# A two-layer FoX and RetNet trunk on one core: accumulator banks and small tiles handed over at other blocks, and a few vector operations fewer

## The chip, the core and the metric

The kernel runs on one core of one Trainium2 chip. The metric is the device time in microseconds (us). An engine is named by its short form: PE is the matrix engine, DVE the vector engine, ACT the scalar engine, POOL GpSimd, SP the engine that issues most DMAs.

## The reference, cut

One sequence of 512 tokens, width 2048, passes two layers; all is fp32.

```python
def fox_branch(x, w_in, b_f, q_gain, k_gain, w_out):
    q, k, v, gate, f_logit = split(x @ w_in)             # 16 heads of 128
    q = rms_norm(heads(q), q_gain); k = rms_norm(heads(k), k_gain)
    c = cumsum(log_sigmoid(f_logit + b_f))               # "forget", per head
    s = q @ k.T * 128 ** -0.5 + c[:, None] - c[None, :]  # causal mask
    return (softmax(s) @ v * silu(gate)) @ w_out

def retention_branch(x, w_in, w_out):
    q, k, v, gate = split(x @ w_in)                      # 8 heads, qk 256, v 512
    q, k = rotary(q), rotary(k) * 256 ** -0.5
    o = retention(q, k, v)                               # decayed chunks of 128 tokens
    return (group_norm_heads(o) * silu(gate)) @ w_out

for i in range(2):
    y = fox_branch(h, ...) if i == 0 else retention_branch(h, ...)
    h = layer_norm(ALPHA * h + y, ln_gain[i], ln_bias[i])
```

## The kernel before

**Products.** An fp32 product is three matmuls (`mm3`, L307 to L309): each operand is split into a high and a low part, the weights by ACT (`w_h`, L302) and DVE (`w_l`, L303). Almost all of the time goes into products of a 512 x 2048 operand with a piece of weights 1024 columns wide ("wide") or 512 ("narrow"). A `Unit` does such a product in Strassen's manner with seven products p1 to p7; a `Plain` unit does it without, in quarters (m, n) (m is the token half, n the column half). Each product is a few blocks: a wide block is 12 matmuls of 128 x 512, a narrow one 24 of 128 x 256. There are 750 blocks; below they are counted from 0 in the order in which PE runs them.

**Accumulators.** PSUM is dealt out by hand: three accumulators of two banks each (`b0` to `b2`, which a unit calls x, y, z) and two small one-bank tiles, `mmp`, for everything else (transposes, scores, a tanh). In a `Unit`, p6, p7 and p4 share x: L457 reads x after p7's last block, and p4 goes on in x after that. p3 has z, read by L452. A tile's next user waits for its last reader.

**Order.** All engines run their instructions in program order, and a planner (`Order`) writes that order. It walks along the list of blocks. Behind each block's matmuls it emits the small steps (generators that `yield need(...)`) that are due: a step is due a given number of blocks after the one before it (`wait`, else 1), when its rings are free (`mmp`, `tmp`, `st` and others are counted with `take` and `give`; `give(ring, 1)` frees it a block later), and while the work booked for DVE and ACT (`debt`) stays under `LIMIT` = 4.4 and 3.8. Weights are loaded up to 9 blocks ahead by SP; the split of a block is emitted three blocks ahead of it, in three buffers.

**What runs where.** Blocks 0 to 15 are a plain narrow unit (q and k of heads 0 and 1), 16 to 43 the first wide unit (`vg[0]`), 44 to 211 nine more such units, narrow (q and k of two heads) and wide (values and gates), with the attention of twelve heads behind them; 212 to 227 a plain narrow unit, 228 to 291 the plain units of FoX's output projection, whose sums are added to the residual by `add_z` (L1373); from 292 on retention, and its output projection to the end. The last unit runs `EARLY`: p4 is cut in two token halves of four blocks each, the "last tokens" second.

Steps that the change touches: `Pair.take` copies a finished narrow quarter (ACT, L956) and takes sums of squares in place (L961); `forget` makes the gates c with 96 matmuls of 16 columns on an `mmp` tile; `silu_twice` (L853, L855) computes a tanh in an `mmp` tile; `head` does a head of attention, transposes of the weights L1035, product L1180, copy by ACT L1186, gate transposes L1190, gating L1193; `rsqrt_steps` is three Newton steps of tiny DVE operations; `first_stores` and `last_stores` normalise and write the output.

## Time and profile before

| what | value |
| --- | --- |
| time, median of 3 runs | 2407.43 us (2407.38 to 2410.28) |
| the profiled execution | 2409.79 us, its span 2408.0 us |
| busy share of the span | PE 97%, DVE 79%, ACT 51%, POOL 6% |
| mean granted clock of PE | 0.992 |
| chain that ended last | PE 71%, DVE 14%, ACT 5%, issue 5%, DMA 4% |

The profiled execution is 1.8 us longer than its span. Views give for each engine when an instruction started, how long it took, how long the engine was idle before it and which instruction ended that idle time. The granted clock is the share of full speed that the throttle gave PE in a stretch; its two levels are 1.2 and 2.4 GHz. Line numbers are those of the kernel before.

### The profile page before, as it was taken

Reading aid. Unit: us, or ns where it says so; the run is one execution under the profiler, and the core shown is the slowest. Engines: PE = TensorE matmul, PEld = TensorE weight load, DVE = VectorE, ACT = ScalarE, POOL = GpSimd, SP = SyncE. Lnnn points to the kernel's source line nnn. Section 1 sums busy time; section 2 is a strip of 40 time slices with the busy share of each in tenths; the row PEclk is TensorE's granted clock in tenths of the full one; section 3 lists DMA queues with packets and bytes.
Section 4 is the critical chain, followed back from the end, with each engine's and each line's share of the span. In section 5 each row is a group of like instructions: output and inputs, shape, how many; then the busy total and the mean of one; then the engine's idle time right before and its main releaser. Section 6 shows DMA issues by size and latency. Waiting matters only on the chain.

```text
span 2408.0 us, 34403 instructions
## 1 busy us (share of the span) xinstructions
PE 2334.7 (97%) x13144; PEld 2023.4 (84%) x13144; DVE 1896.8 (79%) x2506; ACT 1221.5 (51%) x1777; POOL 150.5 (6%) x237
## 2 busy tenths in 40 slices
PE   9999999999999999999999999999999999999995
PEld 9788898789789778878989898888889898777784
DVE  4878778768765556677888888898888889987977
ACT  4546556556555534565453545454544446554543
POOL 0000000000000000000010101010101001011002
PEclk9999999999999999999999999999999999999998
DMA  5445554544544457656585857665665659689777
GB/s 212 140 159 171 179 171 153 185 157 154 177 161 144 141 180 233 220 167 206 197 241 188 243 191 220 204 197 184 209 198 191 211 169 274 208 266 299 240 247 176
DMA packets 185142, 473.27 MB, mean 197 GB/s; under 512 B 18033, under 2 KB 63233, under 8 KB 184465
## 3 DMA queue, kind: packets, MB, share of 16 engines
q1 hardware_dynamic: 161296, 403.42, 50.9%
q0 software_dynamic: 23680, 67.66, 10.6%
q8 instruction: 103, 1.69, 0.3%
q14 instruction: 63, 0.51, 0.1%
HBM read 413.30 MB, written 61.91 MB: 197 GB/s over the span
## 4 chain that ended last, share of the span: by engine, by line
PE 71%; DVE 14%; ACT 5%; issue 5%; DMA 4%; POOL 0%; ACTq 0%; DVEq 0%; SPq 0%; POOLq 0%
PE acc L308 21%; PE acc L307 21%; PE acc L309 21%; DVE w_l L303 5%; DMA w_raw<-in_wide 3%; ACT w_h L302 3%; DVE w_q L551 3%; PE mmp L307 2%; PE mmp L308 2%; PE mmp L309 2%; PE mmp L1180 1%; PE mmp L1035 1%; DVE qk_l L987 0%; DVE w_raw L547 0%; DMA y_s<-ny 0%
## 5 line engine op out<-in xcount | busy, mean ns | idle before, releaser
L307 PE MATMUL acc<-w_h,a 128*128 128x512 f32 (+1 forms) x1616 | 584.5, 362 | 19.8 <-DVE p L457 8.2
L303 DVE TENSOR_TENSOR w_l<-w_raw,w_h 128x1024 fp32r<-128x1024 f32 x337 | 411.7, 1222 | 219.5 <-ACT w_h L302 218.0
L308 PE MATMUL acc<-w_l,a 128*128 128x512 f32 (+1 forms) x1616 | 579.2, 358 | 4.5 <-DVE w_l L303 4.4
L309 PE MATMUL acc<-w_h,a 128*128 128x512 f32 (+1 forms) x1616 | 578.5, 358 | 0.0
L302 ACT ACTIVATE w_h<-w_q 128x1024 fp32r<-128x1024 f32 x344 | 363.4, 1058 | 405.4 <-DVE w_q L551 241.5
L302 ACT ACTIVATE w_h<-w_raw 128x1024 fp32r<-128x1024 f32 x337 | 356.0, 1058 | 376.5 <-PE acc L309 197.8
L303 DVE TENSOR_TENSOR w_l<-w_q,w_h 128x1024 fp32r<-128x1024 f32 x344 | 420.1, 1222 | 95.8 <-ACT w_h L302 90.1
L307 PE MATMUL acc<-w_h,s 128*128 128x512 f32 (+1 forms) x1344 | 490.8, 365 | 1.9 <-ACT w_h L302 1.9
L308 PE MATMUL acc<-w_l,s 128*128 128x512 f32 (+1 forms) x1344 | 486.4, 362 | 6.0 <-DVE w_l L303 5.8
L309 PE MATMUL acc<-w_h,s 128*128 128x512 f32 (+1 forms) x1344 | 485.1, 361 | 0.0
L307 PEld LDWEIGHTS acc<-w_h,a 128*128 128x128 f32 x1616 | 307.7, 190 | 65.5 <-issue 13.4
L308 PEld LDWEIGHTS acc<-w_l,a 128*128 128x128 f32 x1616 | 307.9, 191 | 50.5 <-DVE w_l L303 8.7
L309 PEld LDWEIGHTS acc<-w_h,a 128*128 128x128 f32 x1616 | 307.4, 190 | 44.3
L308 PEld LDWEIGHTS acc<-w_l,s 128*128 128x128 f32 x1344 | 254.4, 189 | 48.3 <-DVE w_l L303 12.6
L309 PEld LDWEIGHTS acc<-w_h,s 128*128 128x128 f32 x1344 | 254.0, 189 | 39.3
L307 PEld LDWEIGHTS acc<-w_h,s 128*128 128x128 f32 x1344 | 254.3, 189 | 38.7 <-ACT w_h L302 2.3
L551 DVE TENSOR_TENSOR w_q<-w_q,w_raw 128x1024 f32<-128x1024 f32 x218 | 265.2, 1220 | 9.7 <-DMA w_raw<-in_wide 7.3
L307 PE MATMUL acc<-a,w_h 128*128 128x256 f32 x464 | 132.2, 285 | 1.2 <-ACT w_h L302 1.2
L309 PE MATMUL acc<-a,w_l 128*128 128x256 f32 x464 | 132.1, 285 | 0.8 <-DVE w_l L303 0.8
L308 PE MATMUL acc<-a,w_h 128*128 128x256 f32 x464 | 131.8, 284 | 0.0
L309 PE MATMUL acc<-s,w_l 128*128 128x256 f32 x448 | 126.7, 283 | 0.0
L308 PE MATMUL acc<-s,w_h 128*128 128x256 f32 x448 | 126.7, 283 | 0.0
(245 smaller groups left out, 2946.1 us busy)
## 6 DMA issues: line engine op xcount, KB each, us to landing
w_raw<-in_wide SPq DMA_DIRECT2D x343, 512.0 KB, 3.7
w_raw<-in_narrow SPq DMA_DIRECT2D x146, 512.0 KB, 3.7
w_q<-in_wide SPq DMA_DIRECT2D x60, 512.0 KB, 4.4
room<-in_wide SPq DMA_DIRECT2D x45, 512.0 KB, 4.3
w_q<-in_narrow SPq DMA_DIRECT2D x26, 512.0 KB, 4.6
y_s<-ny POOLq DMA_DIRECT2D x48, 256.0 KB, 7.3
y_s<-y POOLq DMA_DIRECT2D x40, 256.0 KB, 6.1
room<-in_narrow SPq DMA_DIRECT2D x16, 512.0 KB, 4.8
```

Of the source, the lines that this page charges most:

```text
L302: nc.scalar.activation(h, src, AF.Copy)
L303: nc.vector.tensor_sub(l, src, f32(h))
L307: nc.tensor.matmul(ps, a[0], b[0], start=start, stop=False, skip_group_check=True)
L308: nc.tensor.matmul(ps, a[0], b[1], start=False, stop=False, skip_group_check=True)
L309: nc.tensor.matmul(ps, a[1], b[0], start=False, stop=stop, skip_group_check=True)
L551: nc.vector.tensor_add(u.chain[c], u.chain[c], t)
L1035: nc.tensor.transpose(tp[g][:, at], p[q][0][:, k * P:(k + 1) * P], ident)
L1180: nc.tensor.matmul(ps[:, k * P:], vh[:, k], pT[:, k, k * P:], start=k == 0, stop=k == ST - 1)
```

## The change

- `Plain`, narrow: both column quarters of a token half are handed to their reader when both are done, no longer one by one (`PlainBlock.finish`).
- `vg[0]` alone has the ending p3, p7, p4: its last p7 block goes ahead of its last p3 block ("turned"). The piece of weights that p3 lent to p7 is then loaded at p7 and kept for p3; after a turned block DVE's limit is 2.9.
- Last unit: the last tokens' p4 accumulates in z, no longer in y after the first half's.
- `head`: the gate transposes are a step of their own, a block after ACT's copy (in the same block for the last two pairs of heads).
- `silu_twice` gives its `mmp` tile back a block later; `add_z` adds both token blocks of a quarter behind one block.
- Small operations: two multiplies of a Newton step become one where only one value per partition is treated (two uses, in `last_stores`); the copies of variances ahead of rsqrt are dropped (L1398, L1707); one more of the last stores (s = 3, c = 1) adds its bias on DVE and goes out by SP, no longer by POOL with an accumulating DMA.

```diff
@@ slot
-        self.most = (LIMIT[0], 2.4) if b.p == "p6" and b.last else LIMIT
+        self.most = (LIMIT[0], 2.4) if b.p == "p6" and b.last else (2.9, LIMIT[1]) if getattr(b, "turned", False) else LIMIT
@@ rsqrt_steps
-            nc.vector.tensor_mul(t, dst, dst)
-            nc.vector.tensor_mul(t, t, h)
+            if n == 1:
+                nc.vector.scalar_tensor_tensor(t, dst, h, dst, op0=ALU.mult, op1=ALU.mult)
+            else:
+                nc.vector.tensor_mul(t, dst, dst)
+                nc.vector.tensor_mul(t, t, h)
@@ Unit.run
+            i = order.index(("p3", self.blocks - 1))
+            if order[i + 1:i + 3] == [("p7", self.blocks - 1), ("p4", 0)]:
+                order[i:i + 2] = order[i + 1], order[i]
...
+                turned = p == "p7" and order[i + 1] == ("p3", c) or p == "p3" and order[i - 1] == ("p7", c)
@@ Block.load
+            if self.turned and self.p == "p7":
+                u.lent["p3", self.c] = t = new_raw(u.shape)
+                nc.sync.dma_start(t.rearrange("p a b -> p (a b)"), u.source("22", self.c))
@@ Block.multiply, finish
-            b = "y" if u.early and p == "p4" else BANK[p]
+            b = ("z" if self.again else "y") if u.early and p == "p4" else BANK[p]
...
-                self.u.sink(1, 0, self.u.bank["y"], lambda: self.u.leave("y") if e else None, part=1, es=(e,))
+                self.u.sink(1, 0, self.u.bank["yz"[e]], lambda: self.u.leave("yz"[e]), part=1, es=(e,))
@@ PlainBlock.finish
-            at = self.m, self.n
-            if self.u.left[at] == 0 and at in self.u.bank:
-                self.u.sink(*at, self.u.bank.pop(at), lambda after=0: self.u.leave(*at))
+            u, m = self.u, self.m
+            if u.wide or all(u.left[m, n] == 0 for n in range(2)):
+                for at in ((m, self.n),) if u.wide else ((m, 0), (m, 1)):
+                    if u.left[at] == 0 and at in u.bank:
+                        u.sink(*at, u.bank.pop(at), partial(u.leave_after, at))
@@ silu_twice
-            give("mmp")
+            give("mmp", 1)
@@ head
-            yield need(act=0.5, pe=0.45, tmp=1)
+            yield need(act=0.5, tmp=1)
             y = tmp("o")
             nc.scalar.activation(y, ps, AF.Copy, scale=0.5)
             give("mmp")
+            yield need(pe=0.45, mmp=1, wait=0 if self.quick else 1)
             g = mmp()
@@ add_z
-                        yield need(dve=1.2, until=lambda: (m, n, e) in got and o.now - got[m, n, e][1] >= 2)
+                        yield need(dve=1.2, wait=1 - e, until=lambda: (m, n, e) in got and o.now - got[m, n, e][1] >= 2)
@@ ln_factors (and the same in retain, L1707)
-        var = pool.tile([P, 2], F32, name="ln_var", tag="ln_var", bufs=2)[:, :k]
-        nc.vector.tensor_copy(var, mv[:, :, 1])
-        rsqrt(r, var, k, 1.0, LN_EPS)
+        rsqrt(r, mv[:, :, 1], k, 1.0, LN_EPS)
@@ last_stores
-            if s == 3 and c > 1:
+            if s == 3 and c > 0:
```

The planner turns these few lines into another order of small steps behind blocks 13 to 150, 178 to 205 and 210 to 325. Three places follow; line numbers in rows of the changed kernel are higher by 3 to 23.

ACT behind blocks 13 to 17, the end of the first plain unit, before:

```order
L956 ACTIVATE qk_raw<-acc 128x2x256
L302 ACTIVATE w_h<-w_raw 128x1024
L961 ACTIVATE acc,rms_ss<-acc 128x128 x4
L956 ACTIVATE qk_raw<-acc 128x2x256
L302 ACTIVATE s_624<-raw 128x1024
L302 ACTIVATE w_h<-w_raw 128x1024
L961 ACTIVATE acc,rms_ss<-acc 128x128 x4
L956 ACTIVATE qk_raw<-acc 128x2x256
```

The same place now:

```order
L305 ACTIVATE w_h<-w_raw 128x1024
L305 ACTIVATE s_620<-raw 128x1024
L305 ACTIVATE w_h<-w_raw 128x1024
L978 ACTIVATE qk_raw<-acc 128x2x256 x2
L305 ACTIVATE w_h<-w_raw 128x1024
L983 ACTIVATE acc,rms_ss<-acc 128x128 x8
L305 ACTIVATE w_h<-w_raw 128x1024
L978 ACTIVATE qk_raw<-acc 128x2x256 x2
```

The first quarter's copy no longer stands between the blocks that fill the other half of the same accumulator; both copies come after the last of them.

DVE behind the last blocks of `vg[0]` (38 to 41), before; `u` is the sum that p3's L452 makes, `p` the one that p7's L457 makes:

```order
L925 COPY fg<-fg 16x1
L926 TENSOR_TENSOR fg<-fg 16x511
L452 TENSOR_TENSOR u_1116<-acc,u_1116 128x1024
L551 TENSOR_TENSOR w_q<-w_q,w_raw 128x1024
L303 TENSOR_TENSOR w_l<-w_q,w_h 128x1024
L457 TENSOR_TENSOR p_969<-p_969,acc 128x1024
```

The same place now:

```order
L460 TENSOR_TENSOR p_1067<-p_1067,acc 128x1024
L565 TENSOR_TENSOR w_q<-w_q,w_raw 128x1024
L306 TENSOR_TENSOR w_l<-w_q,w_h 128x1024
L455 TENSOR_TENSOR u_1162<-acc,u_1162 128x1024
L565 TENSOR_TENSOR w_q<-w_q,w_raw 128x1024
```

The read of p7's accumulator stands three operations ahead of that of p3's, behind block 38, and the scan of the forget gates (`fg`) has gone to later blocks.

PE behind the first block of a narrow unit (block 142), at the gate transposes of head 6, before; under it the same transposes now (block 140):

```order
L309 MATMUL acc<-w_h,a_192 128x256
L1035 MATMUL mmp<-ident,p 128x128 x4
L1190 MATMUL mmp<-ident,by_head 128x128 x4
L307 MATMUL acc<-w_h,s_446 128x256
```

```order
L312 MATMUL acc<-w_h,a_385 128x512
L1213 MATMUL mmp<-ident,by_head 128x128 x4
L1057 MATMUL mmp<-ident,p 128x128 x3
L310 MATMUL acc<-w_h,a_418 128x512
```

The gate transposes now stand first behind their block, ahead of the other head's transposes, and the product they belong to was copied a block earlier.

## Rows read from the trace of the kernel before

**Rows 1.** The page: busy time of an engine; chain that ended last.

```profile
PE 2334.7 (97%) x13144; PEld 2023.4 (84%) x13144; DVE 1896.8 (79%) x2506; ACT 1221.5 (51%) x1777; POOL 150.5 (6%) x237
```

**Rows 2.** Waits of PE, 50 to 95 us: line, released by: total us, times, longest.

```profile
PE acc L307 <- ACT qk_raw L956: 2.2, 1, 2.2
PE acc L308 <- DVE w_l L303: 2.0, 3, 1.0
```

**Rows 3.** Timeline of DVE, the end of the first wide unit, and of PE.

```profile
141.58 1.21 DVE L452 TENSOR_TENSOR u<-acc,u 128x1024 f32<-128x1024 f32 x1
...
144.98 1.20 DVE L457 TENSOR_TENSOR p<-p,acc 128x1024 f32<-128x1024 f32 x1
146.33 0.76 PE L307 MATMUL acc<-w_h,a 128*128 128x512 f32 x1 [4.78 <-DVE p L457]
```

**Rows 4.** Stretches: us, busy PE, PEld, DVE, ACT, POOL, granted clock, DMA share, GB/s.

```profile
55.20:60.00 4.80, 4.75 (x26) 4.66 (x27) 3.50 (x3) 2.18 (x4) 0.00 (x0) 0.65 0.70 265
146.30:151.50 5.20, 5.17 (x12) 4.12 (x13) 2.15 (x2) 0.00 (x0) 0.53 (x1) 0.50 0.75 223
301.00:312.00 11.00, 8.52 (x67) 7.83 (x66) 7.72 (x11) 6.07 (x12) 0.00 (x0) 1.00 0.24 70
876.40:880.50 4.10, 4.07 (x12) 3.32 (x13) 2.00 (x3) 0.00 (x0) 0.00 (x0) 0.65 0.62 201
```

**Rows 5.** Instructions on the forget tile: min, median, max ns, first and last start.

```profile
L307 PE MATMUL mmp<-a,wf_parts x24: 276/276/283, 107.0 to 120.6; 128*16 128x256 f32 x24
```

**Rows 6.** Waits of PE, 210 to 320 us, the first two units with heads.

```profile
PE mmp L1035 <- DVE p L855: 1.5, 1, 1.5
PE mmp L1190 <- ACT o L1186: 1.5, 2, 0.7
PE mmp L307 <- ACT pT L1058: 0.9, 1, 0.9
PE mmp L1004 <- DVE o L1193: 0.4, 1, 0.4
```

**Rows 7.** Waits of PE, 400 to 510 us, the next two units with heads.

```profile
PE mmp L307 <- ACT pT L1058: 1.7, 2, 1.5
```

**Rows 8.** Waits of PE, 778 to 790 us (second plain narrow unit) and 868 to 885 us.

```profile
PE acc L307 <- ACT qk_raw L956: 1.6, 1, 1.6
PE acc L307 <- DVE z L1373: 3.1, 1, 3.1
```

**Rows 9.** Timeline of DVE at the first sums of the output projection.

```profile
872.89 0.68 DVE L1373 SCALAR_TENSOR_TENSOR z<-z_in,acc 128x512 f32<-128x512 f32 x1
...
875.61 0.68 DVE L1373 SCALAR_TENSOR_TENSOR z<-z_in,acc 128x512 f32<-128x512 f32 x1
```

**Rows 10.** Groups of DVE by line: count, busy us, mean ns, idle before.

```profile
L1707 DVE COPY gn_var<-gn_mv 128x2 f32<-128x2 f32 x16 | 2.6, 163 | 0.0
```

**Rows 11.** Timeline of PE and DVE at the end: start us, us, instruction.

```profile
2383.43 0.50 PE L307 MATMUL acc<-w_h,a 128*128 128x512 f32 x1 [3.61 <-DVE z L1378]
2383.76 0.39 PE L308 MATMUL acc<-w_l,a 128*128 128x512 f32 x1
2383.99 0.39 PE L309 MATMUL acc<-w_h,a 128*128 128x512 f32 x1
...
2386.57 0.15 DVE L1398 COPY ln_var<-ln_mv 128x1 f32<-128x1 f32 x1
2386.76 0.15 DVE L289 TENSOR_SCALAR rsq_h<-ln_var 128x1 f32<-128x1 f32 x1
...
2390.72 0.68 DVE L1378 TENSOR_TENSOR z<-z,acc 128x512 f32<-128x512 f32 x1
...
2400.64 0.69 DVE L1847 TENSOR_TENSOR z<-z,ln_last 128x512 f32<-128x512 f32 x1
```

**Rows 12.** DMA issues, 2390 to 2410 us: count, KB each, us to landing.

```profile
out<-z POOLq DMA_DIRECT2D x6, 256.0 KB, 5.2
out<-z SPq DMA_DIRECT2D x2, 256.0 KB, 5.1
```

More of the change, by code (lines that the diff above doesn't have):

```diff
@@ L512, in __init__ @@
             self.quarter = None
-            if not self.sums and not shared and p != "p1":
+            self.turned = turned
+            if not self.sums and not shared and p != "p1" and not (turned and p == "p3"):
                 self.quarter = {"p2": "21", "p3": "22", "p4": "21", "p5": "12", "p6": "22", "p7": "12"}[p]
@@ L526, in rings @@
         def rings(self):
-            return dict(q=int(self.chain), st=int(self.quarter is not None))
+            return dict(q=int(self.chain), st=int(self.quarter is not None) + int(self.turned and self.p == "p7"))
         def load(self):
@@ L545, in add @@
             if p == "p7" and not self.sums:
-                other = u.lent.pop(("p3", c))
+                other = u.lent["p3", c]
                 nc.vector.tensor_add(self.t, self.t, other)
-                end_raw(other)
+                if not self.turned:
+                    end_raw(u.lent.pop(("p3", c)))
             elif p in ("p5", "p6", "p4") and not self.sums:
@@ L566, in split @@
             else:
+                if self.turned and p == "p3":
+                    self.t = u.lent.pop((p, c))
                 raw = self.t
@@ L591, in multiply @@
             a = forms[FORM[p]]
-            b = "y" if u.early and p == "p4" else BANK[p]
-            new = u.left[p] == u.blocks and (p in ("p1", "p2", "p5") or b == "y")
-            if new and not self.again:
+            b = ("z" if self.again else "y") if u.early and p == "p4" else BANK[p]
+            new = u.left[p] == u.blocks and (p in ("p1", "p2", "p5", "p4") and b in "yz" or b == "x" and p == "p1")
+            if new:
                 u.bank[b] = u.accumulator(b)
@@ L660, in accumulator, with leave_after @@
             return t if self.wide else t[:, n].rearrange("p (e n) -> p e n", e=2)
+        def leave_after(self, at, after=0):
+            self.leave(*at)
         def leave(self, m, n):
```

10 lines of the change are left out of this document (4 added, 6 removed).

## Prediction

> **What bounds the kernel now.** I read the granted clock and the busy time of the engines first, then the chain that ended last, then PE's waits by what released them, and for each such wait the stretch behind it. PE is busy for 2334.7 of 2408.0 us [rows 1] and carries 71% of the chain. So the end can only come earlier where PE stands still, or runs slowly, for a reason that the change removes, and in the last microseconds, when PE has no work left. PE's pace is the distance of two starts, 0.23 us for 128 x 512 [rows 11], 12 of which make a wide block of 2.72 us; the 0.39 us beside it is a modelled end. A wait as the rows give it is therefore about 0.15 us shorter than what PE loses.
>
> The waits that the change can reach are few and have places. In the first 160 us: 2.2 us for ACT's copy of a quarter and three for late `w_l`, 2.0 us together [rows 2], and one of 4.78 us for L457 [rows 3]. Behind the first and the last PE ran at a granted clock of 0.65 and 0.50, its lower level of 1.2 GHz for part or all of about 5 us [rows 4]. Then the units with heads, each with several waits of 0.4 to 1.7 us [rows 6, 7], with the clock at 1.00 all the same from 301 to 312 [rows 4]. Then two single waits, 1.6 us for the same copy as at the start, 3.1 us for L1373 [rows 8], with a clock of 0.65 behind the second [rows 4]. At the end, 3.6 us for L1378 [rows 11].
>
> **First unit and vg[0], part by part.** *Quarters.* The copy of the first quarter stood between blocks that write the other half of the same accumulator. Now both copies come after the second. The 2.2 us go, and the slow stretch behind them, 4.8 x (1 - 0.65) = 1.7: **3.9**. What is late next: the accumulator is free only when two copies and eight squares are through, but its next user is block 20, four wide blocks or 10.9 us later, so nothing.
>
> *Forget's matmuls.* Because the heads' first copies come later, the planner puts the 96 small matmuls of `forget` behind blocks 21 and 22 instead of 31 and 32. They cost PE the same wherever they stand, about 11 us: from 107.0 to the last start at 120.6 [rows 5] lie all of them and one block of 2.72. But at 21 to 26 PE waited for DVE, and now DVE has those 11 us to catch up: **2.0**. The bounds are 0 and 2.0; I take all, since the catching up is five times the wait.
>
> *p7 ahead of p3.* PE waited for L457 because L452, a load sum and a split stood ahead of it on DVE, three operations, 141.58 to 144.98 [rows 3]. In the new order p7's read stands where L452 stood, ahead of them, and without the two scan operations before it. It is emitted a block earlier, and one more block (p3's last) lies between p7 and p4 on PE. If DVE is as late as it was, p7's read starts where L452 did and ends at 141.58 + 1.2 = 142.8, against p4's turn at 146.33 - 4.78 = 141.55. So between nothing and 1.2 of the 4.8 may stay; I take 0.9, since two scan operations ahead of it are gone, and the slow stretch goes, 5.2 x 0.5 = 2.6: **6.5**. p3's own read is now the late one, but z's next user is a unit away. The move issues two loads of 512 KB at one block, on SP, and every load behind them passes later through three buffers. Blocks are loaded up to nine ahead, which is the cover; without it the cost is between nothing and a block, 2.72. I take nothing. 0.3 go back for DVE's moved norms behind blocks 29 to 37. Sum of the first 160 us: 3.9 + 2.0 + 6.5 - 0.3 = **12.1**, with 8 and 14 as bounds.
>
> **Heads.** In the first two units with heads the rows sum to 4.3 us [rows 6]. Two waits are of the kind that the change is about: L1035's transposes want an `mmp` tile that `silu_twice` still reads (1.5), and the gate transposes L1190 want the copy issued just ahead of them (twice 0.75). The first goes, as the tile is given back a block later and so PE is not sent there early; the second goes, as a block of 2.7 lies between. L1004's 0.4 hangs on the same tile. The heads also move: the first gate transposes from behind block 66 to 75, so the 0.9 of L307 meets other work. I leave 1.3 of small new waits, bounds 0 and 4.3: gain **3.0**. In the two later pairs of units the same three lines recur in the same size, with L307 at 1.7 [rows 7], 5.1 each. There the order up to block 121 is unchanged, so L307's 1.7 stays; one 0.75 stays, since now other transposes (L1004) ask for the copied tile at once; and the gate transposes come behind block 123 on a tile that ACT and DVE must first empty of the next heads' q and k. Nothing in the trace shows that wait. Its nearest rows are 0.4 and 1.5 [rows 6]; I take 1.1, nearer the upper one, since two engines must finish. Left 1.7 + 0.75 + 1.1 = 3.6, gain 1.5 each: **3.1**, bounds -4 and 8. A gate step of its own also holds an `mmp` tile longer, and everything else that PE does outside accumulators is queued behind these two tiles; that is the slower rival below.
>
> **Second plain unit and output projection.** The 1.6 us [rows 8] go as in the first unit, but here block 229 takes the accumulator right behind eight squares; I leave 0.2: **1.4**, bounds 0 and 1.6. `add_z` did the second token block's sum a block later, at 875.61 against 872.89 [rows 9], and PE's next unit waited for it. Behind the first sum of 0.68 and its statistics of about the same, it starts 1.3 earlier, so 3.1 becomes 1.8. Waits of 1.5 left the clock at 1.00 [rows 4, 6], so I let the slow stretch go too, 4.1 x 0.35 = 1.4: **2.7**, bounds 1.3 and 4.5.
>
> **Small operations.** The 16 copies in retention, 2.6 us of DVE [rows 10], cost nothing and bring nothing: PE has no wait there that they end. Without that cover they would be worth 2.6.
>
> **The end.** Here DVE is the path. Its chains of tiny operations and the sums between them follow one another to 2401.3, with pauses only for ACT [rows 11], so PE's 3.6 us wait is for DVE, and taking it away by a bank that has been free since p3 brings PE's end forward, from about 2390.6 (24 matmuls from 2383.43, some slow) to 2385.1, but not DVE's. Its gain alone would be the 0.1 by which the last L1378 stood behind PE [rows 11]. The Newton chains stand on that path: one operation is 0.19 from the next [rows 11], four fewer in each of two chains are 1.5, and the copy in `first_stores` 0.2. Against it, s = 3, c = 1 adds 0.7 on DVE. Net 1.0. Both halves need each other: with the old bank, the first chain's 0.77 would end in a wait for PE. The last stores land 5.1 to 5.2 after their issue [rows 12] by either queue, and one accumulating transfer less leaves the DMA engines 0.2: **1.2**, bounds 0 and 2.5.
> The Trainium skill, "DMA: Bandwidth & Descriptors" (section "Latency and other measured facts"), gives the first byte of a transfer after some 0.6 us by the sequencers' queues and 1 us by GpSimd's; by it the end would gain 0.4 more. The trace shows 0.1 between the two [rows 12], so it is left out of the sum.
>
> **The sum.** 12.1 + 3.0 + 3.1 + 1.4 + 2.7 + 1.2 = 23.5. Some 15 waits disappear, each worth 0.15 more than its row: 2.2. Together 25.7. From the profiled execution, 2409.79, that gives 2384.1; it lies 2.4 above the median of the runs, so against the median of 2407.43 I expect **2381.7**.
>
> **Rivals.** *Heads give nothing back.* The gate transposes only change what they wait for, and the hand-over a block later meets the next user. For it: only two tiles, and all waits of the heads are for them. Against: a block of 2.7 is longer than any of these waits. Then 6.1 is missing: 2388.
> *p7's read is late all the same.* DVE was behind by more than the three operations, as its busy row shows no pause there; then the 6.5 go back: 2388. Against: fewer operations stand ahead of it now.
> *Short waits pull the clock down.* If a row of short waits is enough to bring PE to its lower level, the new order of waits behind blocks 122 to 125 could do it in four units, at 2.6 each (the price at 146 to 151): 10.4, 2392. Against: the waits before were as many, with the clock at 1.00 [rows 4].
> The Trainium skill, "TensorE: Matmul & The Clock Gate" (section "A second HAM failure mode: psum-queue depth-cycling"), describes this: cycling through PSUM banks leaves PE idle so briefly and often that its clock swings between the levels. By that rule the time would be this rival's; the row of 301 to 312 speaks against it.
> *Slower: the two small tiles jam.* The gate step keeps a tile until the block after the copy, in twelve heads. If PE then stands a whole block for a tile (2.72) and the clock falls behind it (2.6), that is 5.3 a head, 64 in all: 2446. It decides from (25.7 + 4.8) / 12 = 2.5 us a head on, more than any wait of the heads in the rows. Against: other steps can go ahead of it in the planner.
>
> **Chances.** Forecast 0.62, heads 0.16, late read 0.08, clock 0.06, several of these together so that it comes within 0.2% (4.8 us, about what a measurement of this kernel can tell from no change) 0.04, jam 0.04. The forecast's own bounds, with heads from -4 and the rest at half, are 2372 to 2391. The range for 8 in 10 is 2371 to 2395, which takes in the first three rivals. Faster by over 0.2%: 0.92; within: 0.04; slower: 0.04.
>
> **What would show it.** Right: no wait of PE for L956's successor, for p7's read at most 1 us, granted clock at 1.00 from 50 to 160 us; forget's matmuls at about 73 to 90; L1190's successor without a wait for ACT's copy in the first units; at the output projection's first sums a wait of about 1.8 with a full clock; at the end PE done 5 us before DVE's last L1378, and DVE's last operation some 15 us behind PE's last matmul. Wrong: a wait of 2 us or more for a new releaser at blocks 20 to 43 or 122 to 125, or a clock under 1.00 in a stretch where it was full.

## The result, and the profile after the change

The changed kernel took **2391.41 us** (median of 6 runs, 2388.19 to 2394.39), the kernel before, run beside it, 2408.86 us (2407.38 to 2415.09). The ratio is 0.9924, interval 0.9911 to 0.9937, so the change saved 15 to 21 us. Forecast were 2381.7 us and a saving of 25.7. The time lies in the range, the direction is right, and about a third of the expected gain is missing. The profiled execution of the changed kernel took 2388.19 us with a span of 2386.4. It is the fastest of the six, 3.2 below the median, so its stages add up to 21.6 us of gain, where the medians differ by 17.5.

The page's first part, busy time of each engine, answers [rows 1]: PE is busy 13.8 us less, with the same number of matmuls.

```profile
PE 2320.9 (97%) x13144; PEld 2016.2 (84%) x13144; DVE 1892.1 (79%) x2480; ACT 1223.0 (51%) x1777; POOL 150.4 (6%) x236
```

To see where the time went I timed each stretch of blocks on PE's timeline, from the start of the first accumulating matmul of one block to that of another. These are distances of two starts, so the modelled ends don't enter. The last column is what the prediction's sum has there. (The first 0.1 of the 21.6 is an earlier start of block 0.)

```
blocks       before    after   change   predicted
  0 to  44   152.13   141.14   -11.0      -12.1
 44 to 104   200.05   202.35    +2.3       -3.0
104 to 212   370.48   367.17    -3.3       -3.1
212 to 250   136.62   136.41    -0.2       -1.4
250 to 262    37.35    34.60    -2.8       -2.7
262 to 330   206.15   206.73    +0.6        0
330 to 726  1211.10  1206.84    -4.3        0
726 to 742    49.91    48.62    -1.3        0
742 to end    35.77    34.26    -1.5       -1.2
(modelled ends of the waits)                -2.2
```

Three places were hit (104 to 212, 250 to 262, the end), two missed by 4 us and more.

**The first 160 us.** Waits of PE in the changed kernel from 100 to 175 us (line, releaser, total, times, longest). The 2.2 us and the 4.78 us of [rows 2, 3] are gone, and from 50 to 95 us only 0.3 is left, but one wait is new:

```profile
PE acc L311 <- DVE w_l L306: 3.6, 2, 2.7
```

DVE's timeline ahead of it, and PE's first matmul behind it (start, length, instruction, idle time before and what ended it), show where it comes from:

```profile
120.88 1.22 DVE L306 TENSOR_TENSOR w_l<-w_raw,w_h 128x1024 fp32r<-128x1024 f32 x1
125.50 1.23 DVE L560 TENSOR_TENSOR w_raw<-w_raw 128x1024 f32<-128x1024 f32 x1 [3.40 <-DMA w_raw<-in_wide]
126.65 1.22 DVE L306 TENSOR_TENSOR w_l<-w_raw,w_h 128x1024 fp32r<-128x1024 f32 x1
...
127.92 0.50 PE L311 MATMUL acc<-w_l,s 128*128 128x512 f32 x1 [2.75 <-DVE w_l L306]
```

L560 at 125.50 is the load sum of the turned p7 (block 38), which needs two loads at once. SP's timeline gives their issues: the line of p3's load first, and four microseconds later the other one, when the split at 120.88 had freed a buffer.

```profile
117.87 0.33 SPq L548 DMA_DIRECT2D w_raw<-in_wide  x1
122.13 0.33 SPq L551 DMA_DIRECT2D w_raw<-in_wide  x1
```

DVE stands still for 3.40 us on the second load, the split of block 37 stands behind the sum in DVE's order, and PE waits for that split.

**The clock.** The stretches that answer [rows 4] (length, busy PE, PEld, DVE, ACT, POOL, granted clock, DMA share, GB/s): behind the first quarter, block 37, the units with heads, and the first sums of the output projection.

```profile
52.80:57.60 4.80, 4.80 (x34) 4.46 (x34) 1.40 (x2) 2.78 (x7) 0.00 (x0) 1.00 0.80 315
124.80:136.00 11.20, 8.45 (x30) 6.53 (x29) 9.94 (x11) 5.82 (x6) 0.00 (x0) 0.85 0.47 154
390.00:500.00 110.00, 105.92 (x542) 86.75 (x541) 83.21 (x140) 62.84 (x114) 5.40 (x10) 1.00 0.49 162
859.00:866.00 7.00, 5.30 (x24) 4.11 (x23) 4.92 (x6) 1.72 (x3) 0.00 (x0) 1.00 0.40 133
```

The clock is full where the quarters were and at the output projection, and under 1.00 behind the new wait of 2.75 us. That last value is one execution's: four of the kernels below have the same wait of 2.7 us at block 37, and over the 6 us behind it the clock is 0.72 in one of them (as here), 0.50 in one and 1.00 in two.

**The units with heads.** PE's waits in the first two of them, which answer [rows 6], 210 to 330 us:

```profile
PE mmp L310 <- ACT pT L1080: 1.6, 1, 1.6
PE mmp L1026 <- DVE sm L1106: 1.3, 1, 1.3
PE mmp L310 <- DVE sm L1106: 0.6, 1, 0.6
PE mmp L1057 <- ACT pT L1080: 0.6, 2, 0.3
```

L1035's wait and the gate transposes' (L1190) have gone as foreseen, but others have come, 5.0 us with the three small ones not shown, against 4.3 and a 0.2 that [rows 6] leave out. In the next two units the lines answer [rows 7]:

```profile
PE mmp L310 <- ACT pT L1080: 1.7, 2, 1.5
PE mmp L1213 <- PE acc L312: 0.9, 1, 0.9
PE mmp L1057 <- ACT pT L1080: 0.8, 3, 0.3
PE mmp L1026 <- ACT o L1208: 0.7, 1, 0.7
```

The gate transposes (L1213) wait 0.9, where the prediction had 1.1. The row names PE's own matmul, but that one had ended at 421.15. What ended the wait stands in DVE's timeline, its second read of a small tile with the next heads' q and k, which is done at 421.94; so it is the wait that the prediction meant, for a tile that ACT and DVE must first empty:

```profile
421.46 0.48 DVE L1009 SCALAR_TENSOR_TENSOR qk_l<-mmp,cols,qk_h 128x256 fp32r<-128x256 f32 x1 [0.54 <-ACT qk_h L1008]
...
422.04 0.63 PE L1213 MATMUL mmp<-ident,by_head 128*128 128x128 f32 x4 [0.89 <-PE acc L312]
```

**Second plain unit and output projection.** Waits of PE from 760 to 870 us, against [rows 8]:

```profile
PE mmp L1017 <- DVE qk_l L1009: 1.7, 1, 1.7
PE acc L310 <- DVE z L1396: 1.7, 1, 1.7
```

The 1.6 us for ACT's copy are gone. The first line is new (block 235): a split of the next activations, 1.23 us on DVE at 801.33, now stands between the q and k tiles that the transposes wait for. The second line is the 3.1 us of before, shortened by 1.4; [rows 9] had 2.72 between the two sums, now it is 1.33:

```profile
860.52 0.68 DVE L1396 SCALAR_TENSOR_TENSOR z<-z_in,acc 128x512 f32<-128x512 f32 x1
861.85 0.67 DVE L1396 SCALAR_TENSOR_TENSOR z<-z_in,acc 128x512 f32<-128x512 f32 x1
```

**The end.** PE's last matmul, DVE's last sum of an accumulator (L1401, which was L1378), two steps of a Newton chain, the first of them fused, and DVE's last operation answer [rows 11]:

```profile
2363.40 0.39 PE L312 MATMUL acc<-w_h,a 128*128 128x512 f32 x1
...
2370.10 0.68 DVE L1401 TENSOR_TENSOR z<-z,acc 128x512 f32<-128x512 f32 x1
...
2372.87 0.22 DVE L297 SCALAR_TENSOR_TENSOR rsq_t<-ln_r,rsq_h 128x1 f32<-128x1 f32 x1
2373.12 0.16 DVE L301 SCALAR_TENSOR_TENSOR ln_r<-rsq_t,ln_r 128x1 f32<-128x1 f32 x1
...
2380.05 0.69 DVE L1866 TENSOR_TENSOR z<-z,ln_last 128x512 f32<-128x512 f32 x1
```

PE is done 6.3 us before L1401 and 17 before DVE; it has no wait for the old bank any more. What the accumulating queue still does behind DVE's last operation (packets, MB, share of the 16 DMA engines), before and after, and then the stores of the last 22 us (count, KB, us to landing), against [rows 12]:

```profile
q0 software_dynamic: 322, 0.57, 49.3%
```

```profile
q0 software_dynamic: 151, 0.27, 31.5%
...
out<-z POOLq DMA_DIRECT2D x5, 256.0 KB, 5.3
out<-z SPq DMA_DIRECT2D x3, 256.0 KB, 4.7
```

### The profile page after: what moved, and what is told of

The parts are those of the page before. It is cut to its first block, busy times and chain, and to the rows that moved or that the text cites. A ratio compares the mean times of both kernels' runs of the same rounds, so it can differ in the third digit from the quotient of the medians.

```text
span 2386.4 us, 34361 instructions
## 1 busy us (share of the span) xinstructions
PE 2320.9 (97%) x13144; PEld 2016.2 (84%) x13144; DVE 1892.1 (79%) x2480; ACT 1223.0 (51%) x1777; POOL 150.4 (6%) x236
## 4 chain that ended last, share of the span: by engine, by line
PE 57%; DVE 8%; issue 3%; DMA 3%; ACT 3%; POOL 0%; ACTq 0%; SPq 0%; DVEq 0%; POOLq 0%
PE acc L311 17%; PE acc L312 17%; PE acc L310 17%; DVE w_l L306 3%; ACT w_h L305 2%; PE mmp L310 1%; DMA w_raw<-in_wide 1%; PE mmp L311 1%; PE mmp L312 1%; DVE w_q L565 1%; DMA v_sum<-in_wide 1%; PE mmp L1202 1%; PE mmp L1736 0%; DMA y_s<-ny 0%; DVE z L1835 0%
```

## The experiments

Twelve kernels were run, nine of them the changed kernel with one step (or three or four) altered, three the kernel before with one step or two added. Ratios are to the kernel before, whose median was 2407.85, 2409.13 and 2408.16 us in the three sets. A profile is one execution, and what the change doesn't touch differs between them by a microsecond or two; so the verdicts rest on stretches and waits first, and on medians where these are far enough apart. The stretches of FoX's units repeat much better: in the seven kernels that have both steps in the heads, blocks 104 to 212 took 366.99 to 367.17 us.

### p7's load sum a block later

```
-        while self.added <= min(i + 3, n - 1):
+        while self.added <= min(i + 3, n - 1) and not (getattr(b := self.line[self.added], "turned", False)
+                                                       and b.p == "p7" and self.added > i + 2):
```

> The changed kernel, but the sum of the turned p7 block on DVE is emitted one block later, behind the weight split of block 37 and no longer ahead of it. All other engines have the same order. Theory A (the new wait of 2.9 us at block 37, with 1.7 of half clock behind it, comes from this sum, which waits for the second of the turned block's two loads while the split that PE needs stands behind it on DVE): the wait at block 37 goes to under 0.5 us, the clock stays full from 120 to 136 us, the span is 3.5 to 4.6 us shorter, and the median 2387. Theory B (the three load buffers are too few once the forget matmuls stand elsewhere, so that some load is late whatever the order): the wait moves to block 38 and stays at 2 us or more, time 2391.

2388.15 us (2387.07 to 2391.59), ratio 0.9920 (0.9905 to 0.9935). The one wait of 2.7 us is gone; from 45 to 175 us PE waits in smaller pieces:

```profile
PE acc L311 <- DVE w_l L306: 2.7, 3, 1.1
PE acc L310 <- DVE p L460: 0.7, 1, 0.7
```

So the place of the sum in DVE's order was the cause of block 37's wait. Blocks 29 to 44 take 45.85 us against 46.85, however: most of the wait came back one and two blocks later, since DVE has a split and a sum for each of these blocks and is late with both. Of some 4.6 us that PE lost at block 37, about 1.0 could be had by the order; the four other kernels that keep the wait have 46.4 to 47.9 us in these blocks, the most where the clock was lowest.

### The old order of p3 and p7

```
-            i = order.index(("p3", self.blocks - 1))
-            if order[i + 1:i + 3] == [("p7", self.blocks - 1), ("p4", 0)]:
-                order[i:i + 2] = order[i + 1], order[i]
```

> The changed kernel with vg[0]'s last blocks in the old order (p3 ahead of p7), everything else as changed. Theory A (the two loads of the turned block made the wait at block 37): no wait at 36 to 38, but p4 waits for p7's read at block 40, between 1 us (DVE is less late than before) and 4.8 us with half a clock of 2.6 behind it; the time then within 3 us of the changed kernel's 2391. Theory B (buffers): the wait of 2.9 us near block 37 stays and the one at block 40 is added, time 2394 to 2398.

2390.91 us (2388.49 to 2394.66), ratio 0.9931 (0.9915 to 0.9948). No wait at block 37, but PE's wait for p7's read is back, from 45 to 175 us:

```profile
PE acc L310 <- DVE p L460: 4.2, 1, 4.2
```

Blocks 29 to 44 take 48.99 us, 2.1 more than in the changed kernel. That is what the turn is worth beside the other steps.

### The quarters handed over one by one

```
-            if u.wide or all(u.left[m, n] == 0 for n in range(2)):
-                for at in ((m, self.n),) if u.wide else ((m, 0), (m, 1)):
-                    if u.left[at] == 0 and at in u.bank:
-                        u.sink(*at, u.bank.pop(at), partial(u.leave_after, at))
+            at = m, self.n
+            if u.left[at] == 0 and at in u.bank:
+                u.sink(*at, u.bank.pop(at), partial(u.leave_after, at))
```

> The changed kernel, but a plain narrow quarter is handed over as soon as it is done, as before. Forget's matmuls go back behind blocks 31 and 32 and the heads to their old blocks. Theory A (the quarters are what moved everything in the first 320 us): the waits of 2.2 us at block 14 with 1.7 of slow clock, of 2.0 us at 21 to 26, and of 1.6 us at 226 come back, the new one of 1.7 us at 235 goes, the one at block 37 goes; and the first two units with heads, which lose 6.9 us in the changed kernel, fall to 3 us or less, as predicted for heads at their old place. Time 2390 to 2394. Rival B (the gate step brings nothing to these units wherever they stand): they stay at 6 us or more, time 2394 to 2398.

2392.63 us (2391.84 to 2394.43), ratio 0.9937 (0.9923 to 0.9952). Waits from 45 to 175 us:

```profile
PE acc L311 <- DVE w_l L306: 2.6, 5, 1.0
PE acc L310 <- ACT qk_raw L977: 2.2, 1, 2.2
PE acc L310 <- DVE p L460: 1.8, 1, 1.8
```

This is the turn without the merging. Blocks 29 to 44 take 56.30 us against 61.90 before: 5.6 for the turn in its own place, where the prediction had 6.5. The wait for p7's read is 1.8 (predicted 0.9). At block 37 there is no wait, and the turned sum's line has no idle time before it:

```profile
129.64 1.22 DVE L560 TENSOR_TENSOR w_raw<-w_raw 128x1024 f32<-128x1024 f32 x1
```

The second load is late only in company with the merged quarters. They bring forget's small matmuls forward, from [rows 5] to 72.0 to 86.1, and then these blocks follow one another every 2.7 us, where before two of them had such matmuls behind them (104 to 121 us). Blocks 44 to 104 took 198.70 us, 3.7 less than in the changed kernel. The merging, in the unit ahead, costs the units with heads their gain.

### The quarters alone

The kernel before with the merging and nothing else.

```
-            at = self.m, self.n
-            if self.u.left[at] == 0 and at in self.u.bank:
-                self.u.sink(*at, self.u.bank.pop(at), lambda after=0: self.u.leave(*at))
+            u, m = self.u, self.m
...
+            if u.wide or all(u.left[m, n] == 0 for n in range(2)):
+                for at in ((m, self.n),) if u.wide else ((m, 0), (m, 1)):
+                    if u.left[at] == 0 and at in u.bank:
+                        u.sink(*at, u.bank.pop(at), partial(u.leave_after, at))
```

> The kernel before with the merged quarters alone (both halves of a narrow accumulator are handed over together, after the second). Theory A: the merging is what cost the units with heads: it gives back the waits of blocks 14 and 21 to 26 (4.0 us in blocks 13 to 20, and 3 to 4 us net in 20 to 44 with the 11 us of small matmuls that move there), but moves the heads, so that blocks 44 to 104 become 3 us longer than in a kernel with single quarters, and block 235's new wait of 1.9 eats block 226's 1.8. Total 3 to 5 us under the kernel before. Theory B: the heads' waits are of the other steps; then blocks 44 to 104 stay within 1 us of the kernel before's 200.1 and the total is 7 us or more under it.

2400.22 us (2399.0 to 2402.64), ratio 0.9969 (0.9957 to 0.9981): 7.9 us. PE's waits from 45 to 175 us:

```profile
PE acc L307 <- DVE p L457: 4.2, 1, 4.2
```

Blocks 13 to 20 take 4.0 us less and blocks 20 to 44 5.0 less, 9.0 together where the prediction had 3.9 + 2.0. Blocks 44 to 104 take 201.08 us, 1.0 more than before, at the limit that the second theory set: the merging alone does little harm there. More of the harm is in its company with the other steps. At block 235 the new wait is there (1.7 us of PE), and the 1.8 at block 226 is gone: both belong to the merging, and they cancel.

### The two steps in the heads alone

```
-            give("mmp")
+            give("mmp", 1)
...
-            yield need(act=0.5, pe=0.45, tmp=1)
+            yield need(act=0.5, tmp=1)
...
+            yield need(pe=0.45, mmp=1, wait=0 if self.quick else 1)
```

> The kernel before with the two steps in the heads alone (silu_twice's tile back a block later, the gate transposes as a step of their own). The prediction's sum: 3.0 us less in blocks 58 to 104 and 3.1 less in 104 to 212, all else as before: 6.1 under the kernel before. Theory after the earlier runs: the gate step moves waits and gains nothing (without it blocks 104 to 212 took 1.6 us less), and only the later return gives something: 1 to 2 us less in 58 to 104, 1.5 to 3 less in 104 to 212, total 2 to 4 under the kernel before.

2402.69 us (2400.54 to 2407.26), ratio 0.9976 (0.9966 to 0.9985): 5.5 us, the prediction's 6.1 within the interval (3.6 to 8.2). The theory made from the first runs, 2 to 4, was too low. By stretches it is -1.7 in blocks 44 to 104 and -3.5 in 104 to 212. Waits of PE, 210 to 320 us, against the 4.3 of [rows 6]:

```profile
PE mmp L307 <- ACT pT L1058: 0.9, 1, 0.9
PE mmp L1191 <- PE acc L309: 0.8, 1, 0.8
PE mmp L1004 <- ACT o L1186: 0.7, 1, 0.7
PE mmp L1035 <- ACT pT L1058: 0.6, 2, 0.3
```

3.0 are left where the prediction had left 1.3.

### The gate transposes right behind the copy again

The last two lines of the diff above taken back in the changed kernel; the tile of `silu_twice` still comes back a block later.

> The changed kernel with the gate transposes right behind ACT's copy again. Theory A (the step of its own trades one wait for another): the copy's wait of 0.9 us comes back in each of the six units with heads, the 1.06 us for the emptied tile at blocks 123 and 179 goes, and the time is within 3 us of 2391. Rival B (the gate step carries most of the heads' gain): two waits of 0.9 in every unit more and nothing back, time 2396 to 2400.

2387.41 us (2385.22 to 2389.49), ratio 0.9915 (0.9900 to 0.9929). Blocks 104 to 212 take 365.60 us, 1.6 less than in the changed kernel; 44 to 104 are the same (202.21). Waits from 392 to 500 us:

```profile
PE mmp L310 <- ACT pT L1080: 1.7, 2, 1.5
PE mmp L1212 <- ACT o L1208: 1.4, 2, 0.7
PE mmp L1026 <- DVE o L1215: 0.4, 1, 0.4
```

Beside the 1.7 that stays in both, 1.8 are left; with the gate step it was 0.9 + 0.8 + 0.7 = 2.4. A step of its own does end the gate transposes' wait for the copy, but the copied tile then goes to other transposes (L1026), which wait for the copy in their place (0.7), and the gate transposes meet a tile that DVE is still reading (0.9).

### `silu_twice`'s tile back at once

```
-            give("mmp", 1)
+            give("mmp")
```

> The changed kernel, but silu_twice gives its small tile back at once and not a block later. Theory A: the later return is what took L1035's wait of 1.5 us away from the first two units with heads (and some 0.75 in later units); without it blocks 58 to 104 take 1.5 to 3 us more and the whole 2 to 4 us more than the changed kernel. Theory B: the merged quarters have moved the heads, and the wait went for that reason; then blocks 58 to 104 stay at 159.6 within 0.5 us and the whole within 1 us.

2388.28 us (2386.94 to 2391.49), ratio 0.9917 (0.9903 to 0.9932). The first theory is out: blocks 58 to 104 take 158.76 us, 0.9 less than in the changed kernel and not more (the second theory had 0.5 at most), and 104 to 212 take the same as there (367.19). The 1.5 us for that tile do not come back as long as the gate step is in.

### Both taken back, and p7's sum a block later

```
+        while ... and not (getattr(b := self.line[self.added], "turned", False) and b.p == "p7" and self.added > i + 2):
...
-            give("mmp", 1)
+            give("mmp")
...
-            yield need(act=0.5, tmp=1)
+            yield need(act=0.5, pe=0.45, tmp=1)
...
-            yield need(pe=0.45, mmp=1, wait=0 if self.quick else 1)
```

> The changed kernel with three steps taken back or mended: p7's sum a block later, the gate transposes right behind the copy as before, silu_twice's tile given back at once. If their single gains add (1.0 in blocks 29 to 44, 1.6 in 104 to 212, 0.9 in 58 to 104): 3.5 us under the changed kernel, 2387 to 2388. If the heads' waits only change places: within 1 us of the kernel with the first two alone, which would be about 2.6 under the changed one.

2389.72 us (2387.53 to 2394.51), ratio 0.9926 (0.9911 to 0.9941). The single gains do not add: blocks 104 to 212 are at 370.45 us, as in the kernel before, with its two waits (392 to 500 us):

```profile
PE mmp L1057 <- DVE p L877: 1.5, 1, 1.5
PE mmp L1212 <- ACT o L1208: 1.5, 2, 0.7
```

Together the runs fill a table, blocks 104 to 212 in us: neither step 370.5, the gate step alone 367.2, the later tile alone 365.6, both 367.2. Each takes away the wait of 1.5, and the gate step beside the later tile gives 1.6 back. For blocks 44 to 104, without the turn: with single quarters 200.1 without both steps and 198.4 with both; with merged quarters 201.1 and 201.8. With the turn and merged quarters it is 201.6 and 202.3.

### The old order in add_z

```
-                        yield need(dve=1.2, wait=1 - e, until=lambda: ...)
+                        yield need(dve=1.2, until=lambda: ...)
```

> The changed kernel without add_z's earlier sum: the second token block's sum waits for the next block again. Theory A (the prediction's): TensorE's wait at block 251 is for that sum, so it is 3.1 us again and not 1.85, with half the clock behind it, and blocks 250 to 262 take 37.3 us, 2.7 more than in the changed kernel. Theory B: the shorter wait has to do with the other moves in the unit ahead; then these blocks stay at 34.6.

2393.26 us (2388.97 to 2396.23), ratio 0.9937 (0.9922 to 0.9952). PE's first matmul after the wait, in its timeline, and then the stretch behind it:

```profile
864.58 0.77 PE L310 MATMUL acc<-w_h,a 128*128 128x512 f32 x1 [3.10 <-DVE z L1396]
```

```profile
864.00:871.00 7.00, 6.42 (x16) 5.07 (x17) 2.51 (x4) 0.92 (x1) 0.00 (x0) 0.52 0.40 139
```

3.10 us and a clock of 0.52, its lower level nearly throughout, against 1.70 and 1.00 in the changed kernel. Blocks 250 to 262 take 38.86 us, 4.3 more. The step is right in its cause, and the 1.4 of the wait are right in size; the rest is the clock's, and differs. All five kernels with a wait of 3.1 us there ran slowly behind it, three for a part of the 6 us and two throughout, and took 37.4 to 37.6 us and 38.9 for these blocks; all nine with 1.7 us kept the full clock.

### The last tokens' bank alone

The kernel before with the blocks of the last tokens in bank z.

```
-            b = "y" if u.early and p == "p4" else BANK[p]
+            b = ("z" if self.again else "y") if u.early and p == "p4" else BANK[p]
...
-                self.u.sink(1, 0, self.u.bank["y"], lambda: self.u.leave("y") if e else None, part=1, es=(e,))
+                self.u.sink(1, 0, self.u.bank["yz"[e]], lambda: self.u.leave("yz"[e]), part=1, es=(e,))
```

> The kernel before with one part of the change alone: the blocks of the last tokens write into bank z, no longer into y, whose reader they waited for. Theory A (the prediction's): the end is VectorE's, so TensorE's wait of 3.6 us for L1378 goes and TensorE ends some 5 us sooner, while VectorE's last operation stays within 0.3 us of where it was behind the start of block 742; the time is that of the kernel before, less at most 0.3 us. Theory B: TensorE sets the end; then the wait's 3.6 us come off the time too.

2409.2 us (2406.33 to 2411.62), ratio 1.0002 (0.9993 to 1.0011). PE's last matmul and DVE's last operation:

```profile
2381.81 0.40 PE L309 MATMUL acc<-w_h,a 128*128 128x512 f32 x1
...
2398.90 0.69 DVE L1847 TENSOR_TENSOR z<-z,ln_last 128x512 f32<-128x512 f32 x1
```

Measured from the start of block 742, PE is done after 11.67 us instead of 17.17, and DVE after 29.06, where it was 29.08. A wait of 3.6 us was taken away and the time did not change: DVE has the end.

### The copies in the retention put back

```
-                yield from rsqrt_steps(r[i], mv[i][:, :, 1], 2, 1.0, GN_EPS)
+                var = pool.tile([P, 2], F32, name="gn_var", tag="gn_var", bufs=2)
+                nc.vector.tensor_copy(var, mv[i][:, :, 1])
+                yield from rsqrt_steps(r[i], var, 2, 1.0, GN_EPS)
```

> The changed kernel with the 16 copies in the retention put back (a variance copied to a tile of its own ahead of each inverse root). Blocks 330 to 726 took 4.3 us less in the changed kernel than in the one before, where the prediction had nothing. Theory A (the prediction's): the copies are hidden, so these blocks stay within 1 us of the changed kernel's 1206.8, and the 4.3 us are of the run and not of the change. Theory B: the copies stand ahead of operations that TensorE waits for; then these blocks are 2 us or more longer than in the changed kernel.

2390.91 us (2386.40 to 2391.66), ratio 0.9923 (0.9907 to 0.9938). The median says nothing changed, and blocks 330 to 726 took 1210.4 us, 3.6 more than in the changed kernel, which by the letter is the second theory. One profile each does not carry that: the nine kernels without the copies have 1206.8 to 1211.2 in these blocks, the five with them 1209.6 to 1212.5. Block by block they can be told apart. In eight blocks (350, 351, 361, 392, 393, 404, 650, 652) all five profiles with the copies are longer than all nine without, by 0.06 to 0.30 us, 1.2 together. Block 404 has the most, 3.87 to 3.96 against 3.59 to 3.65; PE's wait in it, first without the copies, then with them:

```profile
1328.90 0.50 PE L311 MATMUL acc<-w_l,s 128*128 128x512 f32 x1 [0.25 <-DVE w_l L306]
```

```profile
1328.74 0.50 PE L311 MATMUL acc<-w_l,s 128*128 128x512 f32 x1 [0.50 <-DVE w_l L306]
```

So the copies cost 1.2 us that can be shown; the means of the two groups differ by 2.3. The rest of the 4.3 in the table above is of those executions.

### A mended version

The changed kernel with p7's sum a block later, the gate transposes as before, the merged quarters in the first plain unit only, and add_z's earlier sum in the first column half (`u == 0`) only, which the expectation calls the first token block. The first two edits are shown above; the others are:

```
-            if u.wide or all(u.left[m, n] == 0 for n in range(2)):
-                for at in ((m, self.n),) if u.wide else ((m, 0), (m, 1)):
+            if u.wide or u.n or all(u.left[m, n] == 0 for n in range(2)):
+                for at in ((m, self.n),) if u.wide or u.n else ((m, 0), (m, 1)):
...
-                        yield need(dve=1.2, wait=1 - e, until=lambda: ...)
+                        yield need(dve=1.2, wait=1 - e if u == 0 else 1, until=lambda: ...)
```

> The changed kernel with four steps altered after the first four runs: the sum for p7's read a block later, the gate transposes right behind the copy as in the kernel before, both copies of an accumulator together only in the half of the unit in which they helped (the quarters of the second half one by one as before), and add_z's earlier sum only for the first token block. If the pieces add: 1.0 less in blocks 29 to 44, 1.6 less in 104 to 212 (both seen), 1.5 to 3 less in 44 to 104 (the heads then stand as in the kernel before), about 1.9 less at block 235 if the second unit's split no longer stands between the transposes there. Sum 4 to 8 us under the changed kernel: 2383 to 2387. If instead each move of DVE's and ACT's work only moves the waits, as in blocks 37 to 39: within 2 us of the changed kernel.

**2386.39 us** (2385.09 to 2388.76), ratio 0.9906 (0.9889 to 0.9922), the fastest of all by its median. It is 5.0 us under the changed kernel's median, but the two intervals overlap, so that it beats the kernel before is shown, and that it beats the changed one is likely, not shown. Of its four edits two worked as wanted: blocks 29 to 44 took 45.92 us (-0.9), 104 to 212 365.55 (-1.6). The single quarters in the second unit did not: the heads in blocks 44 to 104 stand at 202.19 as in the changed kernel, because it is the first unit's merging that moves them, and at 226 and 235 one wait replaced the other again. The edit in add_z changed nothing that can be seen (250 to 262 at 34.61).

## Why the prediction was right, and where it was not

**Right.** *Quarters:* 4.0 in blocks 13 to 20 (3.9 predicted), clock full. *Heads 104 to 212:* 3.3 (3.1), with the wait of L1213 at 0.9 (1.1) and the 0.7 at L1004's successor, as said. But the two steps do not share in it: the tile's later return brings 4.9 by itself, and the gate step beside it gives 1.6 back. In the prediction's own terms that step was a small loss too (1.5 go, 0.75 and 1.1 come, in each pair of units), so its sum came out right although both the gain and the loss are larger than it had them. *add_z:* 2.8 (2.7), with 1.70 left of the wait (1.8) and a full clock; the run without it confirms the cause. That the sizes meet so closely is in part luck, since the same wait cost 1.5 more where the clock stayed low for longer. *The bank:* nothing for DVE's end, as said, and PE done 5.5 us sooner (5.5 predicted; the 2390.6 that it starts from is 1.2 late, as PE's last matmul there ends at 2389.4). *The jam and the clock rival* did not come: the stretch 390 to 500 has seven short waits for tiles and a clock of 1.00, and in all fourteen profiles blocks 44 to 212 have 1.00. The rule of the Trainium skill behind the clock rival ("TensorE: Matmul & The Clock Gate", section "A second HAM failure mode: psum-queue depth-cycling") is thus borne out by no run here.

**The first 160 us: right as a sum, wrong in its terms.** 11.0 against 12.1, inside 8 to 14. But the quarters and forget's move are worth 9.0 alone, not 5.9: the step took 2.0 from [rows 2] for the late `w_l`, with 2.0 as its upper bound, where PE lost 3.5 us in four blocks (21, 22, 23 and 26), and it left out that DVE then reaches p7's read 0.6 us sooner and less slow time follows. The turn is worth 5.6 alone, not 6.5. And the two overlap by 3.6. The step that failed is "I take nothing" for the two loads: the cover that it named, loads up to nine blocks ahead, was there only while other work stretched these blocks. The wait to watch for was named in the list of what would make the prediction wrong (2 us or more with a new releaser at blocks 20 to 43), and it came.

**Blocks 44 to 104: wrong by 5.3 us, the largest part of what is missing.** The term 3.0 was sized from the waits that would go, and "I leave 1.3 of small new waits" was too little even for the step alone (3.0 left, 1.7 gained). The prediction saw that the heads move, from block 66 to 75, but took that for a change of place. In the new place the same steps gain nothing and cost 0.7. The other 1.6 of the 2.3 that these blocks became longer are the merging's (1.0, seen alone) and the turn's (0.6, by the run with the old order), for which the sum had nothing here. With merged quarters the heads meet blocks in which ACT and DVE are later with `pT` and `sm`; that these are late because of the splits and sums of those blocks is argued from the rows, not tested. The rival "heads give nothing back" was right for these two units and wrong, on balance, for the four later ones.

**Block 226: -0.2 instead of -1.4.** The wait went, but the step looked for what is next at the same accumulator, and the new wait stands nine blocks on, behind a split that the merging has moved in front of the k tiles.

**The small copies: "cost nothing and bring nothing" was wrong**, by at least 1.2 us. The step looked for a wait of PE that ends with a copy. The copies work at a distance. Ahead of block 404 two of them make all that follows on DVE 0.4 us later, 0.2 for each, and that arrives at PE some 30 us on, in waits for splits up to this block. DVE has two pauses in between, 0.6 and 1.2 us, but both end with a high part that ACT makes from DVE's own sum; they are as long without the copies, and take nothing up.

**The end: 1.5 against 1.2, by other terms.** The Newton chain is 0.6 us shorter, not 0.77, since a fused operation takes 0.22 and the next starts 0.26 behind it, where each of the two that it replaces took 0.19. From the start of block 742 to DVE's end it is 28.6 us, in the nine other kernels with this ending 28.3, against 29.1 to 29.5 in the four with the old one: 0.5 to 0.8 where the sum had 1.0. But the transfers behind it take less: from DVE's last operation to the end of the span 5.7 us, in the other nine 4.5 to 5.4, against 6.3 to 6.7 with the old ending. Over the last 22 us the accumulating queue is as busy as before, 82% and 81% of the DMA engines' time; what differs is what is still under way at DVE's end. With the old ending the last accumulating store is issued 0.9 us ahead of DVE's end, with the new one 2.1 us or more, and the plain store behind DVE's last operation then lands after 3.6 to 4.7 us and not 5.1 to 5.7. The sum had 0.2 for one such transfer less, for which no row was given; the end came some 1.4 sooner. The new bank is not the reason, as alone it left 6.3; that the transfer is, no run shows by itself. The figures of the Trainium skill on first bytes ("DMA: Bandwidth & Descriptors", section "Latency and other measured facts") would have added 0.4, an estimate. The rows have 0.6 between the two queues' landings in the changed kernel (5.3 and 4.7) and 0.1 in the one before, so the queue by itself decides nothing here that a run could show.

**The modelled ends, 2.2.** That PE loses more than a wait's row is right (2.36 where the row has 2.2; 4.94 where it has 4.78), but in the table it lies inside the stretches, and there the missing terms hide it. So the account closes: of 25.7 predicted, 16.0 came outside blocks 330 to 742. 5.3 are missing in blocks 44 to 104, 2.2 are the modelled ends, 1.2 is missing at block 226 and 1.1 in the first 160 us, 0.6 were lost in blocks 262 to 330, for which I have no cause, and the other stretches gave 0.7 more than forecast. The other 5.6 of the profile (330 to 742) are the copies' 1.2 to 2.3 and 1.5 in blocks 734 to 742; for the remaining 2 to 3 there is no cause but the spread of these blocks between executions. The 1.5 are luck with the clock. These blocks take 25.9 us in this profile and in that of the quarters alone, 27.3 to 27.5 in the twelve others. All fourteen have one wait of PE of more than 1 us there, at block 737, of 1.64 us here and of 1.86 to 1.91 in the rest. The 6 us behind it, in this profile and, for one of the twelve, with p7's sum a block later (columns as above):

```profile
2337.40:2343.40 6.00, 5.25 (x22) 4.12 (x23) 5.09 (x5) 2.91 (x3) 3.63 (x6) 1.00 1.07 237
```

```profile
2335.80:2341.80 6.00, 5.21 (x15) 3.91 (x16) 3.80 (x4) 2.18 (x3) 3.62 (x6) 0.72 1.08 249
```

## What to carry to other kernels

Price a step in the order that it will run in, not in the one of the trace: here two steps that were worth 9.0 and 5.6 us alone gave 11.0 together, and one worth 1.7 turned into a loss, because a third step had moved the work around it. Before a cover is counted ("loads are nine blocks ahead"), ask which other part of the same change takes it away. And where an engine is behind for tens of microseconds, count even its smallest operations for whoever waits at the end of that row; a pause in which it waits for work on its own output does not make up for them.

## What the runs showed of the hardware

- A three-operand operation with a 128 x 1 column takes 0.22 us where the same kind with a constant takes 0.16 and a two-tensor one 0.16. Fusing two of the latter saves 0.13, not 0.19.
- PE's clock behind a wait is not given by the length of the wait. It stayed at its full level of 2.4 GHz through the rows of short waits in the heads in all fourteen profiles, and behind the 1.70 us at block 252 in all nine that have it. It went to 1.2 GHz for a while in twelve of the thirteen profiles with 1.86 to 1.91 us at block 737, in three of the five with 2.7 us at block 37, and in all that have 2.2 us at block 15, 3.1 at block 252 or 4.2 to 4.8 at block 40. So one profile's stretch behind such a wait can differ by 1.5 us from the next one's.
- With one of ten accumulating stores fewer in the last microseconds, the end came 4.5 to 5.7 us behind DVE's last operation in all ten kernels that have this ending, and 6.3 to 6.7 in the four that have the old one; alone it was not tried.
